# Strassen's seven block products in the up projections of a hybrid backbone's SwiGLU layers

## The chip, the cores and the metric

The kernel runs on one core of a Trainium2 chip, as one program. The metric is the device time of one execution in microseconds. A time is given as the median of several executions; the profile is of one execution, with its own time. Engines: TensorE (PE in the profile, its weight loads PEld), VectorE (DVE), ScalarE (ACT), GpSimd (POOL) and SyncE (SP), which issues nearly all DMAs.

## The reference

Two layers over 512 latent tokens and 256 context tokens, width 1024. Each layer is half a SwiGLU sub-layer, an attention mixer, and another half SwiGLU sub-layer, each modulated by vectors that come from a conditioning vector, and closed by a layer norm.

```python
def modulate(h, shift, scale):
    return h * (1.0 + scale) + shift

def swiglu(u, w_in, w_out):                 # w_in 1024 x 5632, w_out 2816 x 1024
    a, v = jnp.split(u @ w_in, 2, axis=-1)
    return (jax.nn.silu(a) * v) @ w_out

def ffn_sublayer(h, shift, scale, gate, w_in, w_out, g, b):
    y = swiglu(modulate(h, shift, scale), w_in, w_out)
    return layer_norm(ALPHA * h + FFN_RES * gate * y, g, b)
...
    for i in range(DEPTH):
        m_lat = jnp.split((silu_c @ w_mod[i] + b_mod[i])[:, None, :], N_MOD, axis=-1)
...
        h_lat = ffn_sublayer(h_lat, m_lat[0], m_lat[1], m_lat[2], ffn_w_in[i, 0], ffn_w_out[i, 0], ...)
...
        y_lat, y_ctx = neighborhood_attention(...)      # layer 0; window_gqa in layer 1
...
        h_lat = ffn_sublayer(h_lat, m_lat[6], m_lat[7], m_lat[8], ffn_w_in[i, 1], ffn_w_out[i, 1], ...)
```

Everything is float32. The context tokens go through the same sub-layers, except the last one.

## The kernel before, in words

Tokens lie in the free dimension: eight tiles `z` of 128 channels x 768 tokens hold the residual stream. A matmul of float32 precision is made of three in a shorter format (float32r): an operand x is split into `hi` (a rounded copy) and `lo` = x - hi, and `mm3` (L113 to L116) issues hi x hi, hi x lo and lo x hi into the same PSUM bank. The modulated input is kept split, in `uh` and `ul` (eight tiles each). Weights are streamed: `wunit` (L86) loads 1 MB in four raw quarter tiles of 128 x 512 through SP's queue (three raw buffers), ScalarE casts each to `hi` (L99) and GpSimd subtracts for `lo` (L100), into a ring of nine pairs.

`ffn` (L399) is called four times: 0a, 0b, 1a with two groups of tokens (512 latent, 256 context), and 1b with two groups of 256. The 2816 hidden columns are 22 tiles of 128, worked in eleven chunks of two. A chunk has three units of weights: two up units, each with the 128 `a` and the 128 `v` columns of one hidden tile, and one down unit. `av` (L407) does an up product for one group: `mmk` (L118) runs eight k-tiles times three matmuls for `a` into a bank "mm" and the same for `v` into a bank "c"; then Silu on ScalarE (L418), the product on VectorE (L419), and the split of the result into `gh` and `gl` (L420, L421). `down` (L423) runs for each of eight output tiles two k-tiles times three matmuls into one of three banks ("s", "s", "t"), and VectorE adds gate x result to `z` (`accumulate`, L394, L395). Chunk 0 is intertwined with the layer norm before it; chunk 9 does the first group alone and is repeated for the second group at the end (`late` and "r"); chunk 10 lets the next layer norm start early. Chunks 1 to 8 are the plain ones, called middle chunks here.

Beside the middle chunks runs a matrix-vector product in the background: `gemv_dve` (L155) computes modulation vectors of later stages on VectorE, one `tensor_tensor_reduce` on 128 x 256 per step (L172), with weight tiles `wt` in twelve slab buffers of a pool `sp` that the mixers use as well. `tick` (L192) emits steps: `rate` after each accumulate and before each up product. `behind` puts each step after the last accumulate in VectorE's queue.

The framework's planner turns this program into one fixed queue per engine, by data dependencies, buffers and its own estimate of times; so TensorE's queue has next chunk's up products between the down products of this one, and splits run ahead of their use as far as the ring lets them. At run time each engine takes its queue strictly in that order and waits where an operand or a buffer is not there yet. PSUM banks: "mm" 2, "s" 2, "c" 2, "t" 1, "o" 1.

Of the kernel before, what the change touches and what calls it, by code (L numbers as in the profile page):

```python
# [8 lines left out]
F32 = mybir.dt.float32  # L9
# [9 lines left out]
P = 128  # L19
# [12 lines left out]
SLABS = 12  # L32
RW = 63
# [3 lines left out]
def hybrid_kernel(ctx: ExitStack, tc: tile.TileContext, h0, cc, crow, wmod, wmodt, bmod, lnp, wst,  # L37
# [47 lines left out]

    def wunit(slabs=False, again=None):  # L86
# [4 lines left out]
        for q in range(4):  # L91
            nm = f"{i}_{q}" + ("" if again is None else "b")
            raw = wp.tile([P, 512], F32, tag="wr", name=f"wr{nm}", bufs=3)
            loaded[0] = nc.sync.dma_start(raw[:], wst[i, :, q * 512:(q + 1) * 512])
            if slabs:
                hi, lo = [sp.tile([P, 512], F32R, tag="slab", name=f"w{x}{nm}", bufs=SLABS) for x in "hl"]
            else:
                hi, lo = [wp.tile([P, 512], F32R, tag=f"w{x}", name=f"w{x}{nm}", bufs=9) for x in "hl"]
            nc.scalar.copy(hi[:], raw[:])  # L99
            nc.gpsimd.tensor_tensor(out=lo[:], in0=raw[:], in1=hi[:].bitcast(F32), op=ALU.subtract)  # L100
            hs.append(hi)
            ls.append(lo)
# [15 lines left out]
    def mmk(ps, w, m0, c0, c1):  # L118

        for k in range(DT):  # L120
            mm3(ps, kw(w, k, m0, m0 + P), [t[k][:, c0:c1] for t in (uh, ul)], k == 0, k == DT - 1)
# [23 lines left out]
    def gemv_bg(layer, ch):  # L145
        pieces = []
        for q in range(8):
            t = sp.tile([P, 1, 512], F32, tag="slab", name=f"wm{layer}_{ch}_{q}", bufs=SLABS)
# [6 lines left out]
    def gemv_dve(layer, t0, t1):  # L155

        cb = []

        def start():
            for i in range(4):  # L160
                t = sp.tile([P, 512], F32, tag="slab", name=f"cb{layer}_{t0}_{i}", bufs=SLABS)
                nc.sync.dma_start(t[:], crow[i // 2, i % 2:i % 2 + 1, :].broadcast_to([P, 512]))
                behind(nc.scalar.activation(t[:], t[:], AF.Silu), last_exp[0])
                cb.append(t)

        def products(acc, t, half):
            w = sp.tile([P, 512], F32, tag="slab", name=f"wt{layer}_{t}_{half}", bufs=SLABS)
            nc.sync.dma_start(w[:], wmodt[layer, t, half])
            for st in range(2):
                for q in range(2):  # L170
                    junk = t2(f"jk{layer}_{t}_{half}_{st}_{q}", "ln")
                    x = nc.vector.tensor_tensor_reduce(out=junk[:, 0:256], in0=w[:, q * 256:q * 256 + 256],  # L172
# [226 lines left out]
    def ffn(nm, groups, gt, mid, post, units=(), opened={}, head=None, apart=None):  # L399
# [34 lines left out]
        if mid is not None:  # L434
            mid()
# [673 lines left out]
```

## Time and profile before

| | |
|---|---|
| median of three executions | 2928.74 us (2925.1 to 2929.07) |
| profiled execution: its time | 2926.03 us |
| profiled execution: span from first to last instruction | 2924.2 us |
| mean granted TensorE clock | 0.983 of full speed |
| DMA | 286 MB, 98 GB/s over the span |
| ScalarE busy | 1033.0 us, 35% |

The profile's page gives busy time per engine, groups of instructions by source line (count, busy time, mean duration, and what ended the idle time before them) and DMA. Views of the trace cut this to a stretch of time, to one tile, or to single instructions in order. The shapes behind an arrow are partitions x elements. Matmuls overlap in the array, so the duration of a matmul is more than its share of TensorE's time; the distance from one start to the next is what counts. Over the middle chunks of 0a, 0b and 1a, 576 matmuls run in 100 us; of 1b, 849 do.

### The profile page before, as it was taken

The numbers are of one execution on the slowest core, as the hardware profiler recorded it, in microseconds if no ns is written. First come the engines' busy times: TensorE is split into PE (matmuls) and PEld (weight loads), VectorE is DVE, ScalarE is ACT, GpSimd is POOL, SyncE is SP. The second block draws the span as 40 slices with busy tenths as digits, with TensorE's granted clock in tenths as the row PEclk, the third lists the DMA queues.
The fourth block names the chain that finished last, engine by engine and source line by source line (L and its number), as shares of the span: only waits on it lengthen the run. The fifth ranks groups of instructions, "written<-read, shape, count | busy, mean of one in ns | idle before, by whom it ended". The sixth has DMA issues, their size and how long they took to land. (4 is left out here: it accounts for less than half of the span.)

```text
span 2924.2 us, 49325 instructions
## 1 busy us (share of the span) xinstructions
PE 2802.8 (96%) x18106; PEld 2470.4 (84%) x18106; DVE 1842.5 (63%) x5023; ACT 1033.0 (35%) x2122; POOL 1247.8 (43%) x1102
## 2 busy tenths in 40 slices
PE   8899999989999979999999899999998999899997
PEld 5788888888888869888888788888887777799997
DVE  3489994375545685767675757776358667733335
ACT  4122122266455452222223522121236655533333
POOL 4233232465433563332335623232456544644453
PEclk9999999999999989999999999999999999899998
DMA  7444442232211312343432324342321111233332
GB/s 290 147 148 145 134 138 61 85 89 80 66 50 52 108 60 87 109 126 109 122 96 87 112 87 121 108 125 73 87 85 55 51 37 30 76 94 96 97 108 81
DMA packets 165842, 286.05 MB, mean 98 GB/s; under 512 B 25952, under 2 KB 38368, under 8 KB 164576
## 3 DMA queue, kind: packets, MB, share of 16 engines
q1 hardware_dynamic: 165312, 282.76, 32.1%
q8 instruction: 142, 2.33, 0.3%
q14 instruction: 100, 0.82, 0.1%
q10 hardware_dynamic: 288, 0.14, 0.0%
HBM read 280.74 MB, written 6.48 MB: 98 GB/s over the span
## 5 line engine op out<-in xcount | busy, mean ns | idle before, releaser
L100 POOL TENSOR_TENSOR wl<-wr,wh 128x512 fp32r<-128x512 f32 x632 | 834.4, 1333 | 1226.7 <-ACT wh L99 1002.3
L99 ACT CAST wh<-wr 128x512 fp32r<-128x512 f32 x632 | 388.9, 620 | 738.4 <-DMA wr<-in_wst_dram 324.4
L172 DVE CUSTOM_DVE_ANT_0 jk<-wt,cb 128x256 f32<-128x256 f32 x960 | 489.3, 544 | 0.0
L395 DVE SCALAR_TENSOR_TENSOR z<-pd1a,gt,z 128x512 f32<-128x512 f32 (+1 forms) x168 | 103.0, 619 | 89.8 <-PE pd1a L116 89.6
L395 DVE SCALAR_TENSOR_TENSOR z<-pd0a,gt,z 128x512 f32<-128x512 f32 (+1 forms) x168 | 102.9, 618 | 83.9 <-PE pd0a L116 83.4
L395 DVE SCALAR_TENSOR_TENSOR z<-pd0b,gt,z 128x256 f32<-128x256 f32 (+1 forms) x176 | 105.0, 600 | 76.6 <-PE pd0b L116 76.5
L114 PE MATMUL pa0a<-uh,wh 128*128 128x512 f32 (+1 forms) x328 | 113.8, 347 | 14.8 <-ACT wh L99 10.9
L114 PE MATMUL pd0a<-gh0a,wh 128*128 128x512 f32 (+1 forms) x336 | 114.9, 345 | 2.9 <-DVE z L395 2.9
L114 PE MATMUL pd0b<-gh0b,wh 128*128 128x256 f32 (+1 forms) x352 | 116.7, 334 | 0.3 <-DVE z L395 0.3
L115 PE MATMUL pd0b<-gl0b,wh 128*128 128x256 f32 (+1 forms) x352 | 116.7, 332 | 0.0
L116 PE MATMUL pd0b<-gh0b,wl 128*128 128x256 f32 (+1 forms) x352 | 116.6, 332 | 0.0
L114 PE MATMUL pa1a<-uh,wh 128*128 128x512 f32 (+1 forms) x336 | 114.7, 341 | 1.2 <-DVE uh L259 1.2
L114 PE MATMUL pd1a<-gh1a,wh 128*128 128x512 f32 (+1 forms) x336 | 113.7, 342 | 1.3 <-DVE z L395 0.7
L114 PE MATMUL pv1a<-uh,wh 128*128 128x512 f32 (+1 forms) x336 | 114.6, 341 | 0.0
L115 PE MATMUL pv1a<-ul,wh 128*128 128x512 f32 (+1 forms) x336 | 114.5, 341 | 0.0
L115 PE MATMUL pa1a<-ul,wh 128*128 128x512 f32 (+1 forms) x336 | 114.3, 340 | 0.0
L116 PE MATMUL pd0a<-gh0a,wl 128*128 128x512 f32 (+1 forms) x336 | 114.3, 341 | 0.0
L115 PE MATMUL pd0a<-gl0a,wh 128*128 128x512 f32 (+1 forms) x336 | 114.3, 340 | 0.0
L116 PE MATMUL pv1a<-uh,wl 128*128 128x512 f32 (+1 forms) x336 | 114.2, 340 | 0.0
L115 PE MATMUL pd1a<-gl1a,wh 128*128 128x512 f32 (+1 forms) x336 | 114.2, 340 | 0.0
L116 PE MATMUL pa1a<-uh,wl 128*128 128x512 f32 (+1 forms) x336 | 114.2, 340 | 0.0
L116 PE MATMUL pd1a<-gh1a,wl 128*128 128x512 f32 (+1 forms) x336 | 114.0, 340 | 0.0
(882 smaller groups left out, 9238.2 us busy)
## 6 DMA issues: line engine op xcount, KB each, us to landing
wr<-in_wst_dram SPq DMA_DIRECT2D x632, 256.0 KB
wt<-in_wmodt_dram SPq DMA_DIRECT2D x240, 256.0 KB
wm<-in_wmod_dram SPq DMA_DIRECT2D x8, 1024.0 KB
nb<-yd SPq DMA_DIRECT2D x60, 128.0 KB
wr_0b<-in_wst_dram SPq DMA_DIRECT2D x19, 256.0 KB
wr_1b<-in_wst_dram SPq DMA_DIRECT2D x19, 256.0 KB
wr_2b<-in_wst_dram SPq DMA_DIRECT2D x19, 256.0 KB
wr_3b<-in_wst_dram SPq DMA_DIRECT2D x19, 256.0 KB
```

The lines of the kernel that those rows point to most:

```text
L99: nc.scalar.copy(hi[:], raw[:])
L100: nc.gpsimd.tensor_tensor(out=lo[:], in0=raw[:], in1=hi[:].bitcast(F32), op=ALU.subtract)
L114: nc.tensor.matmul(ps, a[0], b[0], start=first, stop=False)
L115: nc.tensor.matmul(ps, a[0], b[1], start=False, stop=False)
L116: nc.tensor.matmul(ps, a[1], b[0], start=False, stop=last)
L172: x = nc.vector.tensor_tensor_reduce(out=junk[:, 0:256], in0=w[:, q * 256:q * 256 + 256], in1=cb[2 * st + half][:, q * 256:q * 256 + 256], ...
L395: last[0] = nc.vector.scalar_tensor_tensor(out=zt(d, c0, c1), in0=pd, scalar=gt[:, d, st:st + 1], in1=zt(d, c0, c1), op0=ALU.mult, op1=ALU ...
```

## The change

In the middle chunks, the up product of a unit is written as a 2 x 2 block product: the weights A are cut in `a` and `v` columns times two halves of the contraction (k-tiles 0 to 3 and 4 to 7), the input B in the same two halves of the contraction times even and odd blocks of 128 tokens. Strassen's method (in Winograd's form) gets the four result blocks from seven block products in place of eight. Each product is four k-tiles of three matmuls with 384 columns (three blocks of 128 at a stride of 256; 256 columns in 1b).

The sums of the input are made once per FFN, after chunk 0 (`sums`): x1, x2 and x3 go, split, into tiles of a new pool; x4 takes the place of one block of `uh` and `ul`, which is saved to DRAM and brought back after chunk 8 (`restore`). The sums of the weights are made for each unit (`quarters`): s1, s2 on VectorE, s3, s4 on GpSimd, so seven pairs are split per unit in place of four. `seven` issues the products and combines them from PSUM on ScalarE, VectorE and, once, GpSimd. After each unit `tick(2 * rate)` is called, after each accumulate `tick(rate)`. In 1b's middle chunks `down` takes all 512 tokens as one group.

To make room: the ring has 8 pairs instead of 9, raw tiles are 5 instead of 3; the slab pool lives only outside the middle chunks ("S"), and a pool "T" only inside; the background gemv works on 512 columns per step, with two buffers for `wt`, half of the contraction after the other, and one addition at the end for all tiles in place of three small operations per tile; the two gate products at the start take their weights through the six `t2` buffers. The late chunk starts its contraction with k-tile 4. Where chunk 0 does its groups apart, its down unit is loaded again too.

```diff
+RING = 8
+RAWS = 5
...
     def gemv_dve(layer, t0, t1):
+        def products(t, half, cb):
+            w = ph["T"].tile([P, 512], F32, tag="wt", name=f"wt{layer}_{t}_{half}", bufs=2)
             nc.sync.dma_start(w[:], wmodt[layer, t, half])
             for st in range(2):
-                for q in range(2):
-                    junk = t2(f"jk{layer}_{t}_{half}_{st}_{q}", "ln")
-                    x = nc.vector.tensor_tensor_reduce(out=junk[:, 0:256], in0=w[:, q * 256:q * 256 + 256],
...
+                junk = t2(f"jk{layer}_{t}_{half}_{st}", "ln")
+                x = nc.vector.tensor_tensor_reduce(out=junk[:], in0=w[:], in1=cb[st][:], scale=1.0, scalar=0.0,
+                                                   op0=ALU.mult, op1=ALU.add, accum_out=acc[:, t - t0, half, st:st + 1])
+                behind(x, last[0])
+                yield
...
-        bg.append((8 * (t1 - t0), steps()))
+        bg.append((4 * (t1 - t0), steps()))
...
+        def sums():
+            saved = dp.tile([2, 4, P, n2], F32, name=f"sv{nm}")
+            for j in range(4):
+                for x, t in enumerate((uh, ul)):
+                    nc.sync.dma_start(saved[x, j].rearrange("p (a b) -> p a b", b=P), half(t[j], 1).bitcast(F32))
+                x1, x2, x3, x4 = [t2(f"x{nm}_{j}_{i}")[:, 0:n2] for i in range(4)]
...
+                k = j + 4
+                op(nc.vector, x1, (uh[j], 1), (uh[j], 0), ALU.subtract)
+                op(nc.vector, x1, x1, (ul[j], 1), ALU.add)
+                op(nc.vector, x1, x1, (ul[j], 0), ALU.subtract)
+                op(nc.gpsimd, x3, (uh[k], 1), (uh[j], 1), ALU.subtract)
+                op(nc.gpsimd, x3, x3, (ul[k], 1), ALU.add)
+                op(nc.gpsimd, x3, x3, (ul[j], 1), ALU.subtract)
+                op(nc.vector, x2, (uh[k], 1), x1, ALU.subtract)
+                op(nc.vector, x2, x2, (ul[k], 1), ALU.add)
+                op(nc.vector, x4, x2, (uh[k], 0), ALU.subtract)
+                op(nc.vector, x4, x4, (ul[k], 0), ALU.subtract)
+                for i, x in enumerate((x1, x2, x3)):
...
+                    nc.scalar.copy(hi, x)
+                    nc.vector.tensor_tensor(out=lo, in0=x, in1=hi.bitcast(F32), op=ALU.subtract)
+                    ts[i][j] = [as_half(hi), as_half(lo)]
+                nc.scalar.copy(half(uh[j], 1), as_half(x4))
+                nc.vector.tensor_tensor(out=half(ul[j], 1), in0=as_half(x4), in1=half(uh[j], 1).bitcast(F32), op=ALU.subtract)
...
+        def quarters():
...
+            out = [pair("a11", a11), pair("a12", a12)]
+            s1 = tt(nc.vector, 1, a21, a22, ALU.add)
+            s2 = tt(nc.vector, 2, s1, a11, ALU.subtract)
+            out += [pair("s2", s2), pair("s1", s1)]
+            s4 = tt(nc.gpsimd, 4, a12, s2, ALU.subtract)
+            s3 = tt(nc.gpsimd, 3, a11, a21, ALU.subtract)
+            return out + [pair("s4", s4), pair("s3", s3), pair("a22", a22)]
...
+        def seven(un, gh, gl):
...
+            def product(n, tag, b):
+                ps = bank(tag, f"p{n}{un}")
+                for k in range(4):
+                    mm3(as_half(ps[:, 0:n2]), [t[:, k * P:(k + 1) * P] for t in w[n]], b[k], k == 0, k == 3)
+                return ps[:, 0:n2]
...
+            nc.scalar.copy(va, product(0, "mm", b11))
+            op(sa, product(1, "o", b21), va)
+            nc.scalar.activation(sa, sa, AF.Silu)
+            op(va, product(2, "mm", ts[1]), va)
+            nc.scalar.copy(vb, product(3, "c", ts[0]))
+            op(sb, va, vb, eng=nc.gpsimd)
+            op(sb, product(4, "c", b22), sb)
+            nc.scalar.activation(sb, sb, AF.Silu)
+            op(va, product(5, "mm", ts[2]), va)
+            op(vb, va, vb)
+            op(va, va, product(6, "o", x4), ALU.subtract)
+            for h, (v, x) in enumerate(((va, sa), (vb, sb))):
+                op(v, v, x, ALU.mult)
+                nc.scalar.copy(half(gh, h), as_half(v))
+                op(half(gl, h), as_half(v), half(gh, h).bitcast(F32), ALU.subtract)
...
+            if not r and 0 < ci < NCH - 2:
+                gs = [[gp.tile([P, NT], F32R, tag="gs", name=f"g{x}{nm}_{ci}_{i}", bufs=6) for x in "hl"] for i in range(2)]
+                for i in range(2):
+                    seven(f"{nm}_{ci}_{i}", *gs[i])
+                    tick(2 * rate)
+                w = [None, None, wunit()]
+                if ci == NCH - 3:
+                    restore(saved)
+                for g in ([(0, NL, 0)] if nb == 2 else groups):
+                    down(w[2], f"{ci}", gs, g, True)
...
+            if ci == 0:
+                phase("T")
+                saved = sums()
```

137 lines of the change are left out of this document (90 added, 47 removed).

## The prediction

> **What bounds the kernel now.** I read the page first, for the engines' shares and the costliest groups.
>
> ```profile
> span 2924.2 us, 49325 instructions
> PE 2802.8 (96%) x18106; PEld 2470.4 (84%) x18106; DVE 1842.5 (63%) x5023; ACT 1033.0 (35%) x2122; POOL 1247.8 (43%) x1102
> ...
> L100 POOL TENSOR_TENSOR wl<-wr,wh 128x512 fp32r<-128x512 f32 x632 | 834.4, 1333 | 1226.7 <-ACT wh L99 1002.3
> L99 ACT CAST wh<-wr 128x512 fp32r<-128x512 f32 x632 | 388.9, 620 | 738.4 <-DMA wr<-in_wst_dram 324.4
> ```
>
> TensorE looks like the bound, but these are averages over unlike stages. So I took the stretches that hold only middle chunks, one in each of the four FFNs (0a, 0b, 1a, 1b in this order).
>
> ```profile
> core 0: us, PE busy (x) PEld busy (x) DVE busy (x) ACT busy (x) POOL busy (x), PEclk, DMA share, GB/s
> 200.00:400.00 200.00, 198.00 (x1138) 173.68 (x1137) 182.20 (x658) 43.35 (x80) 64.97 (x48) 1.00 0.46 139
> 1200.00:1400.00 200.00, 200.00 (x1151) 175.96 (x1150) 146.91 (x481) 44.25 (x80) 63.94 (x48) 1.00 0.39 116
> 1800.00:2000.00 200.00, 200.00 (x1152) 175.92 (x1151) 144.77 (x480) 45.02 (x80) 63.47 (x48) 1.00 0.39 116
> 2600.00:2800.00 200.00, 200.00 (x1696) 200.00 (x1696) 73.34 (x142) 60.92 (x117) 89.12 (x70) 1.00 0.32 93
> ```
>
> A middle chunk has 288 matmuls (192 up, 96 down), half of 512 columns and half of 256. By the counts of these rows it takes 50.6 us in 0a, 50.0 in 0b and 1a, 34.0 in 1b, where all have 256 columns. The mean step from one matmul to the next is 200/1151 = 0.174 us, and 200/1696 = 0.118 us in 1b. TensorE has no idle time there, so what the change takes off TensorE comes off the end, if no other engine takes its place. In 0a VectorE is 91% busy, in 0b and 1a 73%; why that is so shows in the next rows, of 0a and of 0b, and in the least, median and greatest time of the same operation.
>
> ```profile
> L172 DVE CUSTOM_DVE_ANT_0 jk<-wt,cb 128x256 f32<-128x256 f32 x236 | 113.5, 517 | 0.0
> L395 DVE SCALAR_TENSOR_TENSOR z<-pd0a,gt,z 128x512 f32<-128x512 f32 x31 | 23.1, 744 | 2.4 <-PE pd0a L116 2.1
> L395 DVE SCALAR_TENSOR_TENSOR z<-pd0a,gt,z 128x256 f32<-128x256 f32 x32 | 15.3, 477 | 4.7 <-PE pd0a L116 4.7
> L187 DVE TENSOR_SCALAR mod<-ga,bmod_sb 128x2 f32<-128x2 f32 x29 | 12.3, 423 | 0.2
> L185 DVE TENSOR_TENSOR ga<-ga 128x4 f32<-128x4 f32 x29 | 8.8, 303 | 0.1
> L186 DVE TENSOR_TENSOR ga<-ga 128x2 f32<-128x2 f32 x29 | 7.7, 267 | 0.2
> ```
> ```profile
> L172 DVE CUSTOM_DVE_ANT_0 jk<-wt,cb 128x256 f32<-128x256 f32 x160 | 81.0, 538 | 0.0
> L421 DVE TENSOR_TENSOR gl0b<-sl0b,gh0b 128x256 fp32r<-128x256 f32 x8 | 11.5, 1436 | 5.8 <-ACT gh0b L420 5.8
> L185 DVE TENSOR_TENSOR ga<-ga 128x4 f32<-128x4 f32 x20 | 5.8, 290 | 0.1
> ```
> ```profile
> L172 DVE CUSTOM_DVE_ANT_0 jk<-wt,cb x236: 405/415/1510, 199.8 to 399.7; 128x256 f32<-128x256 f32 x118
> ```
>
> Over the whole span, the same kind of operation with one operand in PSUM:
>
> ```profile
> L419 DVE TENSOR_TENSOR sl0a<-pv0a,sl0a 128x512 f32<-128x512 f32 x22 | 15.1, 686 | 34.0 <-PE pv0a L116 33.9
> L419 DVE TENSOR_TENSOR sl1b<-pv1b,sl1b 128x256 f32<-128x256 f32 x42 | 17.8, 424 | 100.0 <-PE pv1b L116 95.6 <-ACT sl1b L418 4.4
> ```
>
> A product of the background gemv takes 0.415 us, yet its mean is 0.517: some take 1.5. The timeline of VectorE and of GpSimd at one place shows what these wait for.
>
> ```profile
> 1807.10 0.47 DVE L395 SCALAR_TENSOR_TENSOR z<-pd1a,gt,z 128x256 f32<-128x256 f32 x1
> 1808.54 1.50 DVE L172 CUSTOM_DVE_ANT_0 jk<-wt,cb 128x256 f32<-128x256 f32 x1
> 1810.39 0.41 DVE L172 CUSTOM_DVE_ANT_0 jk<-wt,cb 128x256 f32<-128x256 f32 x1
> 1810.73 0.41 DVE L172 CUSTOM_DVE_ANT_0 jk<-wt,cb 128x256 f32<-128x256 f32 x1
> 1811.08 0.15 DVE L186 TENSOR_TENSOR ga<-ga 128x2 f32<-128x2 f32 x1
> 1811.84 0.21 DVE L187 TENSOR_SCALAR mod<-ga,bmod_sb 128x2 f32<-128x2 f32 x1
> ```
> ```profile
> 1807.01 1.32 POOL L100 TENSOR_TENSOR wl<-wr,wh 128x512 fp32r<-128x512 f32 x1 [0.47 <-PE pv1a L115]
> ```
> ```profile
> 1808.28 1.47 POOL L100 TENSOR_TENSOR wl<-wr,wh 128x512 fp32r<-128x512 f32 x1
> ```
>
> The product of 1808.54 reads two tiles in SBUF and ends at 1810.04, 0.29 us after GpSimd's split ends at 1809.75: it had to wait for it. The accumulate of 1807.10, which reads PSUM and SBUF, ran through a split in its usual 0.47. So a GpSimd tensor_tensor stops VectorE's operations on two SBUF tiles, and not those that read PSUM. The price per split in 0a: 236 x (0.517 - 0.415) = 24.1, L187 29 x (0.423 - 0.21) = 6.2, L185 and L186 29 x (0.303 + 0.267 - 0.30) = 7.8, together 38 us over 48 splits, **0.79 us**. In 0b: 160 x (0.538 - 0.415) = 19.7, L185 20 x (0.290 - 0.15) = 2.8, L421 8 x (1.436 - 0.424) = 8.1, together 30.6 over 48, **0.64 us**.
>
> **TensorE.** A unit has 96 up matmuls, 48 x 768 columns; seven products of four k-tiles by three terms are 84 of 384 columns (256 in 1b). 384 is the mean of 512 and 256, so a step is 0.174. A chunk is 168 + 96 = 264 steps: 45.8 us. In 1b down becomes one group, 48 steps of 512 columns at 2 x 0.174 - 0.118 = 0.23, so 168 x 0.118 + 48 x 0.23 = 30.9. Over eight chunks that would take 39 us off 0a, 34 off 0b, 34 off 1a and 25 off 1b: 132 us. I take three blocks of 128 as no dearer than a row of 384; were each 128 as dear as a 256-column step, 0.354, the method would lose outright, but nothing in the rows suggests it.
>
> **GpSimd.** Splits go from 12 to 18 per chunk (seven per unit in place of four, four for down). Added are two weight sums and one 384-column sum per unit: 24 operations for 12.
>
> ```profile
> L100 POOL TENSOR_TENSOR wl<-wr,wh 128x512 fp32r<-128x512 f32 x36 | 46.0, 1294 | 56.0 <-ACT wh L99 37.5 <-PE pv1b L115 12.4 <-PE pv1b L116 4.1
> L283 POOL TENSOR_TENSOR aql<-aql,sql 128x256 f32<-128x256 f32 x16 | 12.4, 773 | 22.2 <-ACT sql L361 21.9
> ```
>
> That is 22 x 1.294 + 2 x about 1.05 = 30.6 us per chunk: room under 45.8, hardly any under 30.9 (22 x 1.294 + 2 x 0.8 = 30.1 there). ScalarE has 18 casts of 0.62 and six copies or Silus per unit of at most 0.62: under 19 us, so it binds nowhere.
>
> **VectorE, without waits.** The next operation starts about 0.07 before one ends (1810.39 to 1810.73 is 0.34 for 0.41). Per chunk: 16 accumulates, 8 x (0.67 + 0.41) = 8.6. Per unit ten operations on 384 columns, five with PSUM and five on SBUF alone, each between 0.424 and 0.686, so 0.555 less 0.07: 20 x 0.485 = 9.7. Two weight sums per unit on 512 columns: 4 x 0.615 = 2.5. Together 20.8. A gemv product has now 512 columns: 0.415 + (0.686 - 0.424) = 0.677, less 0.07, 0.61. There are 192, 160 and 128 of these in 0a, 0b, 1a (half as many as before), at 40 per chunk in 0a (rate 2) and 20 in 0b and 1a (rate 1); the three small operations per modulation tile go.
>
> **With waits.** 24 operations of GpSimd at 0.64 to 0.79 are 15.4 to 19.0 us; I take 0.70, 16.8, about the middle, since the share of two-SBUF work stays near that of 0b while VectorE is as full as in 0a.
> - 0b: 20.8 + 12.2 + 16.8 = 49.8 (48.4 to 52.0) against TensorE's 45.8: VectorE is late next. Eight chunks 398, before 400: -2 (-13 to +16).
> - 0a: 4.8 chunks with products, 20.8 + 24.4 + 19.0 = 64.2, and 3.2 at TensorE's 45.8, are 455; spread evenly, 166 + 117 + 192 x 0.70 = 417. I take 436, halfway, as VectorE's order is planned ahead but late products slip; before 405: +31 (+12 to +50).
> - 1a: 6.4 x 49.8 + 1.6 x 45.8 = 392, before 400: -8 (-17 to +6).
> - 1b: GpSimd 30.1, and the 14 two-SBUF operations of VectorE, each of which can hold it up by 0.29 (256 columns, as above) to 0.55 (512), at most 5.1: 30.9 to 35.2, taken at 32.5. 260, before 272: -12 (-25 to +9).
> Sum +9.
>
> On this the Trainium skill ("SBUF — State Buffer", section "SBUF: two separate sides") says that the pair of ports shared by VectorE and GpSimd is an exclusive lock, kept for the whole instruction, also by a VectorE operation with two SBUF inputs. The trace agrees that one blocks the other; but 0.29 us after the split for an operation of 0.41 says that not all of it is held up. By the rule taken whole, the time would be that of the third rival below.
>
> **Beside the chunks.** Before the first Strassen chunk, 44 VectorE operations (44 x 0.485 = 21 us), 12 of GpSimd and 16 of ScalarE form sums and splits. Down of chunk 0 covers most: 96 steps are 16.7 us (11 in 1b). What must come after chunk 0's last up matmul is four casts and four subtractions of x4, about 4 us. Were none covered, 21 us per FFN; I take 5, so 20 us (0 to 84). Eight saves and eight restores per FFN go through SP's queue, past the weight loads.
>
> ```profile
> SPq L168 <- DVE ga L172: 447.2, 164, 5.8
> ```
> ```profile
> L168 SPq DMA_DIRECT2D wt<-in_wmodt_dram x20: 327/328/328, 1312.8 to 1396.4; - x20
> ```
>
> 16 x 0.33 = 5 us of issue, covered by raw tiles that are five deep. The gemv's weight tile falls from a share of twelve slabs to two of its own: VectorE never waited for it (idle 0.0 in L172), but SP did wait for VectorE. If a load arrives late, the accumulates queue behind the product and TensorE behind their banks: nothing to 60 us (480 products are 240 tiles, by 0.25 us each). Bank "o" takes products 2 and 7 of a unit, so VectorE must have emptied the seventh within one product of the next unit, 12 x 0.174 = 2.1 us; a gemv product of 1.50 ahead of it in the queue still leaves room for one operation. Ring 8 for 9 and six tiles for twelve under the first gate's gemv shorten loads ahead; chunk 0 of 0b and 1b loads and splits its down weights twice, 4 x 1.33 us of a GpSimd that is otherwise a third busy. None can gain, since buffers only fall; I take 6 for all. The other order of k in the late chunk costs nothing, its cover is chunk 8's down, 16.7 us for eight restores. Together +9 + 20 + 6 = +35. The profiled run took 2926.03 us, 1.8 beyond its span and 2.7 under the median of 2928.74: **2961 us**.
>
> **Rivals.**
> 1. *TensorE stays the bound* (faster). For it: in 0a VectorE is 91% busy and TensorE lost only 1%, so a nearly full VectorE costs little. Against: the waits grow with GpSimd's work. It decides where a GpSimd operation costs VectorE about 0.53: there 0b needs 20.8 + 12.2 + 12.8 = 45.8, so 0b and 1a give -34 each, 0a evenly spread 385, -20, 1b -15: -103, with the 26 beside 2849. At 0b's own 0.64 it is 0a +17, 0b -13, 1a -17, 1b -12: 2927. The rival is what lies between, its middle 2888.
> 2. *The weight tile's two buffers*: 60 for 6, and sums uncovered, 84 for 20: 2961 + 118 = 3079. For it: SP's 447 us on these products. Against: VectorE has never waited for a landing yet.
> 3. *The two engines line up one after the other*, each operation in its full duration: 0b 30.6 + 10 x 0.555 + 4 x 0.686 + 20 x 0.677 = 52.4, 419; 0a 4.8 x 66.0 + 147 = 463; 1a 409; 1b 30.1 + 10 x 0.424 + 4 x 0.686 = 37.1, 297. That is 1588 for 1477: +111 + 26, 3063. Against it: the 0.29.
> 4. *No saving*: a moving operand in three blocks costs more than 0.174. At 0.20 TensorE's chunk is 50.3, and 0b, 1a and 0a's light chunks follow: about 2980.
>
> **How the numbers follow.** Forecast 0.45 (its own range 2915 to 3005), rival 1 0.34, rival 2 0.08, rival 3 0.10, rival 4 0.03. The range 2860 to 3050 leaves out the best part of rival 1, most of rival 2 and half of rival 3, together under 2 in 10. About 0.2%, 6 us, is what a measurement of this kernel can tell from no change. Faster 0.36: rival 1, and 0.02 from the forecast's low edge; same 0.07, from that edge too; slower 0.57, all else.
>
> **What would show it.** Right: in 0b VectorE over 95% busy, TensorE 90 to 97% instead of 100, chunks of 47 to 52 us, 0a's first five chunks near 60, L172's successor with a mean far over 0.677, 1b's GpSimd over 90%. Wrong: middle chunks of 46 us in 0b with TensorE at 100% (rival 1), product waits that end on a DMA (rival 2), chunks over 52 (rival 3), steps over 0.18 us with no idle time (rival 4).

## The result and the profile after

| | before | after |
|---|---|---|
| median (four executions each) | 2928.55 us | 3155.01 us (3148.95 to 3161.61) |
| profiled execution: time, span | 2926.03, 2924.2 us | 3161.61, 3159.8 us |
| mean granted TensorE clock | 0.983 | 0.945 |

The ratio is 1.0776 (95% interval 1.0752 to 1.0801): slower by 226 us, where 32 were forecast and at most 121 allowed for. First the page of after: the engines' line, and its three costliest groups, which answer to the product and to most of the splits of before.

```profile
span 3159.8 us, 48012 instructions
PE 2825.9 (89%) x16954; PEld 2497.9 (79%) x16954; DVE 2330.5 (74%) x4333; ACT 1216.5 (38%) x2514; POOL 1895.8 (60%) x1542
...
L98 POOL TENSOR_TENSOR wl<-wr,wh 128x512 fp32r<-128x512 f32 x376 | 515.7, 1389 | 316.1 <-ACT wh L97 273.6
L187 DVE CUSTOM_DVE_ANT_0 jk<-wt,cb 128x512 f32<-128x512 f32 x480 | 502.6, 1066 | 8.5 <-DMA wt<-in_wmodt_dram 4.3
L98 POOL TENSOR_TENSOR wl_s<-S,wh_s 128x512 fp32r<-128x512 f32 x256 | 379.8, 1504 | 87.8 <-ACT wh_s L97 82.3
```

PE has 1152 matmuls fewer and is yet busy 23 us longer, at a lower granted clock. VectorE is busy 488 us more, GpSimd 648. A product that takes 0.67 us alone has a mean of 1.066. Now the stretches that hold the eight middle chunks of 0a, 0b, 1a and 1b, in this order:

```profile
core 0: us, PE busy (x) PEld busy (x) DVE busy (x) ACT busy (x) POOL busy (x), PEclk, DMA share, GB/s
140.00:612.00 472.00, 394.55 (x2045) 359.07 (x2044) 396.86 (x686) 128.41 (x238) 279.01 (x191) 0.93 0.41 119
1250.00:1678.00 428.00, 394.71 (x2073) 358.61 (x2072) 369.18 (x605) 129.43 (x244) 280.07 (x196) 0.94 0.40 113
1871.00:2294.00 423.00, 391.13 (x2067) 358.01 (x2068) 358.45 (x572) 130.35 (x245) 285.49 (x196) 0.95 0.38 108
2776.00:3062.00 286.00, 260.75 (x1722) 236.83 (x1723) 192.53 (x252) 120.61 (x246) 252.89 (x198) 0.98 0.34 98
```

A chunk takes about 60 us in 0a (480 with the part of the first one ahead of this stretch), 53.4 in 0b, 52.9 in 1a, 35.7 in 1b, where 45.8 (30.9 in 1b) is TensorE's own work. In 0b no engine is full: PE 92% at 0.94 of its clock, VectorE 86%, GpSimd 65%. From the starts of the matmuls in 0b's stretch, some 360 us are steps at full rate, 15 to 20 are what steps at half the clock take more, and 45 to 50 are waits (how a step that is both slow and late is divided is a matter of choice). Against before, the middle chunks are 138 us longer (75, 27, 23, 13); the rest of the loss, about 100, lies outside them, above all between chunk 0 and the first block products.

Where VectorE's time goes in 0b, by groups (busy, mean):

```profile
L187 DVE CUSTOM_DVE_ANT_0 jk<-wt,cb 128x512 f32<-128x512 f32 x148 | 151.2, 1034 | 2.6 <-ACT cb L198 1.9 <-DMA wt<-in_wmodt_dram 0.7
...
L538 DVE TENSOR_TENSOR gl0b<-y0b,gh0b 128x384 fp32r<-128x384 f32 x32 | 41.7, 1328 | 0.1
L538 DVE TENSOR_TENSOR y0b<-y0b,y0b 128x384 f32<-128x384 f32 x32 | 37.6, 1181 | 1.0
L538 DVE TENSOR_TENSOR y0b<-y0b 128x384 f32<-128x384 f32 x16 | 18.3, 1147 | 0.9
L509 DVE TENSOR_TENSOR S<-wr,wr 128x512 f32<-128x512 f32 x15 | 14.1, 942 | 14.9 <-DMA wr<-in_wst_dram 14.9
L509 DVE TENSOR_TENSOR S<-S,wr 128x512 f32<-128x512 f32 x15 | 12.0, 800 | 0.4
...
L538 DVE TENSOR_TENSOR y0b<-p10b,y0b 128x384 f32<-128x384 f32 x15 | 8.2, 546 | 0.0
```

All six groups with two SBUF operands are stretched; the one that reads PSUM (p10b) is not: its mean is 0.546. With 0.55 us taken for 384 columns, 0.615 for a weight sum and 0.672 for a product, the excess is 148 x 0.362 + 32 x 0.778 + 32 x 0.631 + 16 x 0.597 + 15 x (0.327 + 0.185) = 116 us of standing still, for 196 operations of GpSimd: 0.59 us each. How it hits TensorE is seen at the end of one unit, in the timeline of VectorE and GpSimd:

```profile
1500.91 0.55 DVE L538 TENSOR_TENSOR y0b<-p50b,y0b 128x384 f32<-128x384 f32 x1
1501.56 0.72 DVE L538 TENSOR_TENSOR y0b<-y0b 128x384 f32<-128x384 f32 x1
1501.83 1.58 POOL L509 TENSOR_TENSOR S<-wr,wr 128x512 f32<-128x512 f32 x1
1502.39 1.44 DVE L538 TENSOR_TENSOR y0b<-y0b,y0b 128x384 f32<-128x384 f32 x1
1503.38 4.70 POOL L98 TENSOR_TENSOR wl_s<-S,wh_s 128x512 fp32r<-128x512 f32 x3
1503.75 0.54 DVE L538 TENSOR_TENSOR y0b<-y0b,p60b 128x384 f32<-128x384 f32 x1
1504.32 1.06 DVE L538 TENSOR_TENSOR y0b<-y0b,y0b 128x384 f32<-128x384 f32 x1
1505.31 3.18 DVE L538 TENSOR_TENSOR gl0b<-y0b,gh0b 128x384 fp32r<-128x384 f32 x2
```

Seven operations that need about 3.5 us take 7.6. The accumulates and the next unit's evacuations stand behind them in VectorE's queue. TensorE's longest waits in 0b's stretch (us in total, times, longest) are of that kind:

```profile
PE p10b L136 <- DVE y0b L538: 15.1, 13, 2.3
PE pd0b L137 <- DVE gl0b L538: 4.1, 7, 0.6
```

The first is bank "o": product 2 of a unit (its tile is `p1`, counted from 0) waits until VectorE has emptied product 7 (`p6`) of the unit before.

### The profile page after: what moved, and what is told of

Its sections match the earlier page's. It is cut to its first block, busy times and chain, and to the rows that moved or that the text cites. A ratio compares the mean times of both kernels' runs of the same rounds, so it can differ in the third digit from the quotient of the medians.

```text
span 3159.8 us, 48012 instructions
## 1 busy us (share of the span) xinstructions
PE 2825.9 (89%) x16954; PEld 2497.9 (79%) x16954; DVE 2330.5 (74%) x4333; ACT 1216.5 (38%) x2514; POOL 1895.8 (60%) x1542
## 3 DMA queue, kind: packets, MB, share of 16 engines
q1 hardware_dynamic: 288320, 296.40, 32.5%
## 4 chain that ended last, share of the span: by engine, by line
PE 52%; DVE 30%; issue 7%; DMA 5%; POOL 3%; ACT 3%; SPq 1%; DVEq 0%; POOLq 0%; ACTq 0%
DVE jk L187 8%; DVE z L411 3%; DMA wr<-in_wst_dram 3%; DVE y0b L538 2%; DVE y1a L538 2%; PE pd0b L137 1%; PE pd1a L137 1%; DVE S L509 1%; DVE y1b L538 1%; PE pd1a L138 1%; PE pd0b L138 1%; PE wo L697 1%; DVE y0a L538 1%; PE pd1a L136 1%; PE o L697 1%
## 5 line engine op out<-in xcount | busy, mean ns | idle before, releaser
L98 POOL TENSOR_TENSOR wl<-wr,wh 128x512 fp32r<-128x512 f32 x376 | 515.7, 1389 | 316.1 <-ACT wh L97 273.6
L187 DVE CUSTOM_DVE_ANT_0 jk<-wt,cb 128x512 f32<-128x512 f32 x480 | 502.6, 1066 | 8.5 <-DMA wt<-in_wmodt_dram 4.3
L98 POOL TENSOR_TENSOR wl_s<-S,wh_s 128x512 fp32r<-128x512 f32 x256 | 379.8, 1504 | 87.8 <-ACT wh_s L97 82.3
L98 POOL TENSOR_TENSOR wl_a<-wr,wh_a 128x512 fp32r<-128x512 f32 x192 | 276.3, 1443 | 222.6 <-ACT wh_a L97 170.9
L97 ACT CAST wh<-wr 128x512 fp32r<-128x512 f32 x376 | 226.4, 619 | 236.4 <-DMA wr<-in_wst_dram 41.1
L97 ACT CAST wh_s<-S 128x512 fp32r<-128x512 f32 x256 | 155.8, 619 | 325.6 <-DVE S L509 100.1
L97 ACT CAST wh_a<-wr 128x512 fp32r<-128x512 f32 x192 | 118.2, 619 | 198.4 <-issue 58.9
L509 POOL TENSOR_TENSOR S<-wr,S 128x512 f32<-128x512 f32 x64 | 85.7, 1340 | 123.2 <-DVE S L509 92.5
L509 DVE TENSOR_TENSOR S<-wr,wr 128x512 f32<-128x512 f32 x64 | 68.1, 1065 | 82.3 <-DMA wr<-in_wst_dram 82.3
L704 POOL TENSOR_SCALAR p<-p,l 128x512 f32<-128x512 f32 x64 | 44.5, 697 | 118.7 <-DVE l L802 108.6
```

Of the source, the lines that this page charges most:

```text
L97: nc.scalar.copy(hi[:], src[:])
L98: nc.gpsimd.tensor_tensor(out=lo[:], in0=src[:], in1=hi[:].bitcast(F32), op=ALU.subtract)
L187: x = nc.vector.tensor_tensor_reduce(out=junk[:], in0=w[:], in1=cb[st][:], scale=1.0, scalar=0.0, op0=ALU.mult, op1=ALU.add, accum_out=acc ...
L509: eng.tensor_tensor(out=t[:], in0=a[:], in1=b[:], op=o)
L704: nc.gpsimd.tensor_scalar(out=p, in0=p, scalar1=r, scalar2=0.0, op0=ALU.mult, op1=ALU.add)
```

## The experiments

Times in us, each of one execution beside before on the same chip (2922.92 to 2929.65 there); the stage columns, from the traces, run from the start to the first `pq`, from the first `pa0b` to the first `pa1a`, from there to the first `vw`, and from the first `pa1b` to the end of the last matmul. The four executions of after lie 12.7 us apart and those of before on the several chips 6.7, so a difference of some 10 us between two single runs says little.

| kernel | time | 0a | 0b | 1a | 1b |
|---|---|---|---|---|---|
| before | 2928.55 | 615 | 569 | 569 | 404 |
| after | 3155.01 | 720 | 625 | 613 | 439 |
| e1 no sums of the input | 3070.84 | 685 | 604 | 589 | 428 |
| e2 product 7 in bank c | 3133.72 | 717 | 606 | 600 | 448 |
| e3 no background products | 2944.86 | 617 | 564 | 565 | 439 |
| e4 before, no background products | 2914.73 | 607 | 576 | 567 | 403 |
| e5 no GpSimd in weight splits | 2883.80 | 641 | 540 | 545 | 394 |
| e8 products spread evenly | 3095.98 | 680 | 619 | 592 | 441 |
| e9 old up projection in the new frame | 2953.36 | 638 | 577 | 570 | 401 |
| e10 before, splits done twice | 3038.20 | 682 | 592 | 588 | 404 |
| e11 before, no GpSimd in splits | 2895.71 | 604 | 563 | 563 | 401 |
| e12 = e2 + e8 | 3087.55 | 685 | 609 | 588 | 443 |
| e13 = e1 + e2 + e3 | 2849.29 | 590 | 542 | 537 | 418 |
| e14 products with one operand | 3006.59 | 652 | 574 | 570 | 445 |
| e15 = e2 + operand in PSUM | 3094.93 | 699 | 590 | 586 | 457 |
| e16 = e15 + e8 + slabs for the first gate | 3030.58 | 631 | 596 | 584 | 454 |
| e17 = e16 + sums under chunk 1 | 3020.63 | 640 | 601 | 577 | 442 |
| e18 = e16 without the sums | 2930.19 | 609 | 565 | 560 | 432 |
| e19 = e16, products in down only | 3041.04 | 637 | 602 | 587 | 451 |

**First round: the sums, the bank, the products.** After the result my theory was that three things stack up: the sums of the input stand uncovered (A), bank "o" chains two units (B), and the products meet more of GpSimd (C). The rival to C was that the block method costs as much without them.

```diff
e1:
-                saved = sums()
+                ts[i][j] = [half(t[j], 0) for t in (uh, ul)]   # for each i, j
e2:
-            op(va, va, product(6, "o", x4), ALU.subtract)
+            op(va, va, product(6, "c", x4), ALU.subtract)
e3, e4:
-        bg.append((4 * (t1 - t0), steps()))
+        nc.vector.memset(acc[:], 0.01)
```

> Leaves out the sums of the input: no x1 to x4, no save and no restore; the products read the plain blocks of uh and ul, and everything else stays. Theory A (the four transitions from chunk 0 to the first Strassen chunk are exposed, because 44 VectorE operations per FFN stand in VectorE's queue between the accumulates of chunk 0's down): TensorE's idle and slow-clock time there, some 20 to 35 us per FFN, goes, so 70 to 110 us less than 3155, near 3065; the middle chunks stay at 53 us in 0b and 1a. Rival (the transition is late for other reasons, the layer norm before it or the first weights): under 25 us less, above 3130.

> One word changed: the seventh product of a unit goes to a bank of the pair c instead of the single bank o. Theory B (TensorE waits at the second product of the next unit for VectorE to empty the seventh out of the same bank; these waits add up to 15 us in 0b, 11 in 1a, 8 in 0a, 2 in 1b): 20 to 36 us less than 3155, and the waits of p1 on y go. Rival (VectorE is what is late, and the wait moves to the next bank that it must empty): within 10 us of 3155.

> Leaves out the background matrix-vector products on VectorE and the loads of their weights; the modulation vectors that they give are constants. To be compared with the kernel before without the same products. Theory C (VectorE and GpSimd together are too full in the middle chunks): 0b's and 1a's middle chunks fall from 53 us to 46 to 47, 0a's from 60 to 46 to 48, 1b's stay at 35.6; in all about 160 less, 2995, which is still above the kernel before without them, by the transitions. Rival (banks and order cost the same whatever VectorE has to do): middle chunks stay above 50 us, 3090 or more.

> The kernel before without the same background products: the measure for the run without them in the changed kernel. Theory C and its rival expect the same, since TensorE had no idle time in the middle chunks: 2900 to 2929, up to 10 us less in 0a.

84, 21 and 210 us went away, against the median of after. Before, the same edit as e3's took 8 us off (2922.92 on that chip). e3's 210 is more than the 160 expected, e2's 21 is the low end of what was expected, with 1b 9 us longer. So the products cost 8 us before and some 200 in the new kernel, where there are half as many of twice the width. Without them the block method is 30 us slower than before, not 226. Yet GpSimd's hold on VectorE is still there: a stretch of e3's 0b, and the group that ends a unit in it.

```profile
1145.00:1515.00 370.00, 367.18 (x2089) 347.81 (x2088) 239.30 (x313) 130.41 (x241) 262.38 (x195) 1.00 0.27 77
```
```profile
L517 DVE TENSOR_TENSOR gl0b<-y0b,gh0b 128x384 fp32r<-128x384 f32 x32 | 46.3, 1484 | 3.4 <-PE pd0b L137 3.3
```

The subtraction stands longer than in after (1.484 for 1.328), and TensorE waits only 2.9 us of the 370.

**Who makes them dear.** In e5 the splits' low halves leave GpSimd; e11 does that to before. e10 gives before as many GpSimd operations as the new kernel has. e8 moves products from 0a's full chunks to its light ones. e9 keeps the frame and drops the block method.

```diff
e5, e11:
-        nc.gpsimd.tensor_tensor(out=lo[:], in0=src[:], in1=hi[:].bitcast(F32), op=ALU.subtract)
+        nc.scalar.copy(lo[:], src[:])
e8:
-        rate = -(-sum(n for n, _ in bg) // (20 * (NCH - 3)))
+        rate = sum(n for n, _ in bg) / (20.0 * (NCH - 3))      # tick carries the fraction over
e9:
-            if not r and 0 < ci < NCH - 2:
+            if False:
e10 (before, middle chunks only):
+            for _ in range(2):
                 nc.gpsimd.tensor_tensor(out=lo[:], in0=raw[:], in1=hi[:].bitcast(F32), op=ALU.subtract)
```

> The changed kernel, but the low half of every weight split is a plain ScalarE copy of the tile instead of GpSimd's subtraction (so the low half is not the remainder, and the products are not the reference's). GpSimd keeps its three operations per unit. Theory (GpSimd's two-SBUF operations hold up VectorE, and through VectorE's queue TensorE): the middle chunks of 0b and 1a go from 53 us to 46 to 48, those of 0a from 60 to 52 or less, those of 1b from 35.6 to 31 to 32; with some 170 us fewer in all, about 2960 to 3010. Rival (VectorE's own work and TensorE's halved clock after short waits make the chunk, whoever causes the waits): the middle chunks of 0b stay at 51 us or more, and the time over 3090. ScalarE has then 40 copies of 0.6 us a chunk, 25 us, which bounds neither.

> The changed kernel with the background products of the modulation spread evenly over the eight middle chunks of a stage (24 per chunk in 0a, where it was 40 in the first 4.8 chunks; 16 in 1a for 20; 0b is unchanged at 20). Theory (what a product costs grows where VectorE is already full): the middle chunks of 0a take 56 to 58 us in place of 60 on average, 15 to 35 us fewer, 1a 0 to 5 fewer: about 3120 to 3140. Rival (each product costs the same wherever it stands): 3150 to 3160.

> The changed kernel with its smaller rings, its pools by phase, its products of 512 columns on two buffers and its order of the late chunk, but with the middle chunks' up projections done the old way, without block products and block sums. Theory (the loss comes from the block method, not from the housekeeping): 2915 to 2945, as before. Rival (the two buffers of the modulation's weight tile, the ring of eight or the split done twice cost much): over 2960.

> The kernel before, with each GpSimd subtraction of the middle chunks' weight splits done twice (the second gives the same values): 24 operations of GpSimd per chunk in place of 12, as many as the changed kernel has, and nothing else of it. Theory (a GpSimd operation costs a full VectorE about 0.65 us): 0a's chunks with products of rate 2 go from 50.6 to about 58, 20 to 45 us in all; 0b and 1a have VectorE at 44 of 50 us and lose 0 to 15 each; 1b 0 to 10: 2945 to 2990. Rival (GpSimd's work costs VectorE nothing of weight): within 5 us of before. If it is over 3000, GpSimd's operations alone explain most of the loss.

> The kernel before, with the low half of every weight split a plain ScalarE copy in place of GpSimd's subtraction (the low half is not the remainder). It is the control of the same edit in the changed kernel, which went to 2884. Theory (before, TensorE is busy without a break in the middle chunks of 0b and 1a, so GpSimd's hold on VectorE costs it little): 2895 to 2925, and the block method is then worth some 10 to 40 us where GpSimd leaves VectorE alone. Rival (the edit is worth the same to both): under 2800.

e5 went to 2883.8, further than the theory had it, and its control e11 to 2895.7: with GpSimd's splits out of the way the block method is worth 12 us (16 against the runs of before beside them), all overheads paid, which for single runs is hardly clear of their spread. One stretch of e5, nearly eight chunks of 0b, and the group that ends a unit:

```profile
1154.00:1518.00 364.00, 364.00 (x2072) 346.71 (x2071) 276.29 (x606) 205.69 (x392) 60.62 (x48) 1.00 0.45 133
```
```profile
L538 DVE TENSOR_TENSOR gl0b<-y0b,gh0b 128x384 fp32r<-128x384 f32 x32 | 17.7, 555 | 0.5 <-ACT gh0b L556 0.4
```

TensorE has no gap, at full clock, 364/2072 = 0.176 a step; the subtraction is back from 1.328 to 0.555. e10 lost 108, where I expected 60 at most: 66 in 0a, that is 0.69 us for each of 96 added operations, 23 and 19 in 0b and 1a, nothing in 1b, which has no products. This is the price that the prediction took, without any block product. e8 gained 59, more than expected: 40 in 0a, 21 in 1a, where 0 to 5 were expected and nothing here explains the rest. e9 is 24 above before, between theory and rival; by the stages 0a is 23 longer and 0b 8: the frame does cost. One place is the first gate, where TensorE in e9 waited for the weights that now pass through six tiles (us in total, times, longest, from 60 to 110 us; before had no wait there):

```profile
PE gm L155 <- DMA wm<-in_wmod_dram: 2.8, 1, 2.8
```

That line holds only 2.8 of the 23; the rest was not traced to a line.

**The operand.** e14 and e15 ask whether the products cost by their time or by their second SBUF operand. e12 and e13 ask whether the single gains add.

```diff
e14:
-                x = nc.vector.tensor_tensor_reduce(out=junk[:], in0=w[:], in1=cb[st][:], ...)
+                x = nc.vector.tensor_reduce(out=acc[:, t - t0, half, st:st + 1], in_=w[:], axis=AX.X, op=ALU.add)
e15 (with e2; product 2 in bank "s", down in "s", "s", "mm"):
-                    behind(nc.scalar.activation(t[:], t[:], AF.Silu), last_exp[0])
+                    s = bank("to"[st], f"cs{layer}_{t0}_{half}_{st}")
+                    behind(nc.scalar.activation(s[:], t[:], AF.Silu), last_exp[0])
```

> The changed kernel with the seventh product in bank c and the background products spread evenly: both edits compute the same values. If the two gains (21 and 59) stand apart: about 3075. If they remove the same wait, 3090 to 3110. In neither case is it below before.

> The changed kernel without the background products, without the block sums of the input (the products read plain blocks instead), and with the seventh product in bank c: what is left is the seven products, the weights' sums and splits. The products' values are not the reference's. Theory (the saving on TensorE is there, 126 us, and the three things hide it): before without background products was 2915, less 126 and with 24 of the smaller buffers 2813; by adding the three single gains 2840. So 2810 to 2850. Rival (the chunks wait on something else still, such as GpSimd's 24 operations): 2870 or more.

> The changed kernel with each background product replaced by a VectorE sum over the same weight tile, 512 columns, which reads one SBUF operand and writes one column (the modulation's values are not the reference's). The number of operations, their places and their loads stay. Theory (VectorE's operations with two SBUF operands stand still while GpSimd reads; an operation with one does not): the mean of one falls from 1.07 us to 0.55 to 0.70, the middle chunks of 0b from 53 to 47 to 50, 0a's from 60 to 50 to 54, and the time to 3020 to 3090. Rival (it is the products' own time and place in VectorE's queue): the mean stays at 0.9 or more, or the time over 3120.

> The changed kernel with the same products and the same values, but the modulation's broadcast operand (two tiles of 512 columns) lies in two PSUM banks and not in SBUF, so that a background product reads one operand from SBUF and one from PSUM. The two banks come free because product 2 goes to the bank s, product 7 to c, and the down projection of a middle chunk cycles s, s, mm. Theory (VectorE stands still in its operations with two SBUF operands while GpSimd reads): the product's mean falls from 1.07 us to 0.65 to 0.80, the middle chunks of 0b from 53 to 47 to 50, and of 3134 (the kernel with the seventh product in c) 80 to 140 are gone: 2990 to 3055. Rival (the product's own time is what costs): mean over 0.95, or the time over 3100.

e12 kept 67 of 80, between its two expectations. e13 came out 9 above what the single gains add up to, with a 0b in which TensorE never waits:

```profile
1096.00:1468.00 372.00, 372.00 (x2135) 354.59 (x2134) 236.99 (x318) 130.49 (x241) 256.57 (x192) 1.00 0.25 71
```

372/2135 = 0.174 us a step. GpSimd is as busy as in after (69%, where after had 65%), the subtraction that ends a unit takes 1.511 on the mean, and it does no harm where VectorE has slack (64% busy). e14 gave 148 of the 210, 13 us below its range, with a mean of 0.675 for its sum and about 48 us for a chunk of 0b, which supports the theory. e15 keeps the same operation on the same values. The products of after (in 0b) and of e15 (all), least, median and greatest time, and e15's groups at that line:

```profile
L187 DVE CUSTOM_DVE_ANT_0 jk<-wt,cb x148: 672/787/1783, 1251.9 to 1677.0; 128x512 f32<-128x512 f32 x148
```
```profile
L187 DVE CUSTOM_DVE_ANT_0 jk<-wt,cs x480: 666/679/690, 118.1 to 2157.6; 128x512 f32<-128x512 f32 x160
```
```profile
L187 DVE CUSTOM_DVE_ANT_0 jk<-wt,cs 128x512 f32<-128x512 f32 x480 | 314.1, 680 | 33.9 <-DMA wt<-in_wmodt_dram 32.8 <-DVE z L412 0.3 <-DVE ga L187 0.2
L187 DVE DVE_READ_ACCUMULATOR2_ANT ga<- 128x1 f32 x480 | 39.3, 82 | 0.0
```

Not one of the 480 stands still for GpSimd any more, as the theory had it, and yet only 39 us went where 80 to 140 were expected; the middle chunks of 0b went to 50, the upper end. Where the rest stayed, the groups of e15 in its 0b show (from 1228 to 1628 us):

```profile
L539 DVE TENSOR_TENSOR gl0b<-y0b,gh0b 128x384 fp32r<-128x384 f32 x32 | 39.8, 1262 | 3.5 <-ACT gh0b L557 2.6
L539 DVE TENSOR_TENSOR y0b<-y0b,y0b 128x384 f32<-128x384 f32 x32 | 34.9, 1111 | 1.0
```

The operations that end a unit still read two SBUF tiles, and still stand. TensorE's longest waits in that stretch name those, and no background product:

```profile
PE pd0b L137 <- DVE gl0b L539: 8.6, 7, 1.4
PE pd0b L136 <- ACT gh0b L557: 7.6, 7, 2.2
```

That alone does not explain e15, for in e14 the same subtraction takes 1.317 and e14 gained 148. New waits come up as well: VectorE waits 33 us for `wt` and its two buffers, but in e14 it waits 36. What sets e15 apart is TensorE's queue. By the starts of its matmuls in 0b, the other banks made the planner order the products anew: the second products of two units stand together, 24 matmuls, where after and e14 have them apart. 1b, which has no background products, hints at the price of such an order: it takes 457 in e15, 445 in e14 and 448 with bank "c" alone. e14's sum also needs no second instruction to read the accumulator (39 us of VectorE in e15, above). How the 88 us between e14 and e15 divide among these was not tried, so e15 is no clean measure of what the operand is worth. e16 to e19 have e15's banks and its order of the products too.

**A version to keep.** e16 to e19 keep what paid, look for the sums, and for the place of the products.

```diff
e16 (e15, e8 and this):
-            t = t2(f"wm{layer}_{ch}_{q}").rearrange("p (a b) -> p a b", a=1)
+            t = ph["S"].tile([P, 1, 512], F32, tag="slab", name=f"wm{layer}_{ch}_{q}", bufs=SLABS)
e17 (e16 and this; the sums are steps after chunk 1's up products, x4 is formed between its up and down,
     the background products are spread over seven chunks):
-            if not r and 0 < ci < NCH - 2:
+            if not r and 1 < ci < NCH - 2:
e18: e16 with e1's edit
e19 (e16 and this):
-                    tick(2 * rate)
```

> The kernel of the PSUM operand, with the products spread evenly as well and the first gate's weight tiles in twelve slabs again, as before. All edits keep the values. Theory: 30 to 60 below the kernel of the PSUM operand for the even spread (less than the 59 alone, since products are cheaper), 10 to 20 for the first gate: 2935 to 3000. Rival (the sums and GpSimd's other waits leave it there): over 3010.

> The kernel with all three edits, and the sums of the input formed during chunk 1, which is done the old way: its four up products cover the sums that go to tiles of their own, and only the sum that is written in place stands between chunk 1's up and down. Seven chunks instead of eight use the block method, which gives up 16 us of the 126. Theory (the sums cost 84 because nothing covers them): 84 - 16 - 10 to 20 = 45 to 60 below the kernel with all three edits: 2880 to 2950. Rival (covered sums take as much from VectorE elsewhere): within 20 of it or above.

> The kernel with the PSUM operand, the even spread and the twelve slabs (3031), and without the block sums of the input (plain blocks are read instead, so the products' values are not the reference's). Theory (the sums are a term of their own, 84): 2935 to 2955, and what is then left over the kernel without sums and without background products (2849) is the products' own time, 90 to 105. Rival (with less on VectorE the sums cost less): 2965 or more.

> The kernel with the PSUM operand, the even spread and the twelve slabs (3031), with the background products issued between the steps of the down projection alone, and none between the two units of a chunk. The values stay. Theory (a product queued ahead of a unit's evacuations holds their banks and TensorE): 3000 to 3020. Rival (what stays is the chain from a unit's seventh product through the gate to down, and VectorE's total): 3025 to 3050.

e16 gained 64 more, within the 40 to 80 that its two edits were expected to bring, and missed its range by 31, since e15 had missed. e17 gained 10, as the rival had it, no more than two single runs can differ by: under chunk 1 the sums are not free either, and VectorE is 93% busy there. A stretch of e17's chunk 1 in 0b:

```profile
1130.00:1170.00 40.00, 27.25 (x160) 25.00 (x159) 37.37 (x52) 10.43 (x23) 28.45 (x19) 0.79 0.31 93
```

e18 shows the sums at 100 us in e16, a term of their own. It is level with before (2929.34), so in this order of TensorE's queue even a free set of sums would only have broken even with GpSimd's splits where they are. e19 is 10 slower, as its rival had it: the place of the products was not it. No kernel that keeps all the work came below before; e17, the fastest of them with block products, is 3.2% above its run of before.

## Why the prediction was wrong

The direction was right, the size was not: 226 us over the median of before for the 32 forecast (+35 in the sum, which starts at the profiled run). Of the 201 us that the span grew beyond the sum's +35, 129 lie in the middle chunks (138 for +9: 0a 44 over its term, 1a 31, 0b 29, 1b 26) and some 72 beside them (98 for 26). Step by step:

- *TensorE saves 132 us.* Right. The 1152 matmuls fewer are worth 126 at full rate, and the 1323 matmuls with three blocks of 128 in e13's stretch have a mean step of 0.174, which refutes rival 4.
- *A GpSimd operation costs VectorE 0.70.* Right in size: 0.59 in 0b, and 0.69 in 0a of e10. The Trainium skill ("SBUF — State Buffer", section "Who interferes with whom") says that a VectorE instruction with at most one SBUF input, outside the two-port modes, does not contend with GpSimd; e15's 666/679/690 agrees.
- *"VectorE is late next"*, 49.8 us per chunk in 0b. This is the step that failed. VectorE's busy time came out below it (369.2/8 = 46.1) and the chunk above it (53.4). I took the larger of two engines' sums for the chunk's time, as if each could use all its idle time. In after neither could: VectorE and TensorE hand over in fixed order, and in 0b's stretch VectorE waited for TensorE's down products, for weights and for GpSimd's sum (lines below), while TensorE waited for VectorE. The runs show that it takes both loads on VectorE: without the products TensorE waits 2.9 us in e3's stretch, without GpSimd's splits not at all in e5's, with both 45 to 50. So it is not enough that an operation between two units stands: 62 of 0b's 116 us fall on the ends of the units and the weight sums, but these stand as long in e3 and e13 and cost TensorE next to nothing there. Why two loads that leave VectorE 14% idle cannot be fitted in is argued from the fixed order, not shown by a run that changes it. The weights' arrival is not it, since VectorE's wait for them is longer in e5 and e13 (23.2 and 27.7) with TensorE never waiting.

```profile
DVE z L411 <- PE pd0b L138: 25.8, 45, 3.2
DVE S L509 <- DMA wr<-in_wst_dram: 14.9, 5, 3.4
DVE y0b L538 <- POOL y0b L538: 10.6, 3, 7.9
```

- *1b at 32.5 a chunk.* It took 35.7, above the 35.2 taken for the worst, though it has no background products. GpSimd is 88% busy there, and TensorE's longest waits are for the ends of the units (9.9 us for `gl1b`, 5.8 for `gh1b`) and for the splits of the weight sums.
- *0a at 436.* It took about 480: the same fault, with 40 products a chunk on top. I took halfway to the even spread, and e8's 40 us there are what the front-loading costs.
- *"Down of chunk 0 covers most"* of the sums, 5 us per FFN. Wrong: 84 in all by e1, 100 by e18, or 21 to 25 per FFN, as much as none of it covered. The layer norm's operations, chunk 0's accumulates and the sums all want VectorE at that time. From 1790 to 1871 us of after, where the stage 1a begins:

```profile
1790.00:1871.00 81.00, 65.06 (x324) 56.20 (x322) 73.58 (x131) 31.15 (x63) 46.29 (x38) 0.87 0.19 56
```

  VectorE 91% busy, TensorE 80% at a clock of 0.87. The cover that I named was TensorE's time, not VectorE's.
- *6 us for all the rest.* Bank "o" alone is 21 (e2), the frame 24 (e9), most of it in 0a. The bank was reasoned with a product ahead of the evacuation, not with GpSimd stopping the operations ahead of it.
- *Rivals.* 1 fell: VectorE's waits do reach TensorE. 2 is refuted in its mechanism, since the products waited 4.3 us for `wt`, but its 84 for bare sums was right. 3 came nearest in the chunks, 52.4 for 53.4 in 0b, though not because VectorE was busy all that time: it was 86% busy, where the sign for a right forecast was over 95%. No rival added the bare sums to it: 3063 + 64 is 3127.

The sum as it was measured, from after downwards: bank 21, PSUM operand 39, even spread and first gate 64, sums 100: 2930. The last 81, down to e13's 2849, hold the products' own time and what the changed banks and TensorE's other order cost; in 1b, without products, e18 takes 432 and e13 418. e13 is 65 under before without products (2915), of TensorE's 126. The terms depend on their order.

One wait was left alone. GpSimd makes one of the unit's sums, in one queue with its splits, and VectorE waited for it 53.8 us in after (12 times, 8.0 at most). No run gave that sum to VectorE, so what it is worth stays open; in e3's 0b VectorE waited 12.0 us for it and TensorE lost next to nothing.

## What to carry to other kernels

Fewer matmuls buy little if what replaces them goes to the engines that empty TensorE's banks. Where two engines hand work to each other in a fixed order, the larger of their sums is a lower bound for the time, not the time: here 46.1 and 45.8 us of work made chunks of 53.4, and taking either load off VectorE, the products or GpSimd's hold, brought 0b's chunk back to within 1 us of TensorE's own time. A GpSimd operation with SBUF operands cost a VectorE in demand about 0.6 to 0.7 us here, paid by whichever operation with two SBUF operands is next. A cover has to be idle time of the engine that does the covered work. An edit that moves tiles to other banks can reorder a whole queue; the order has to be read from the trace before a gain is put down to the edit.

## What the runs showed of the hardware

The granted clock falls after quite short waits. In 0b of after the longest wait of TensorE from 1256 to 1300 us is 2.4 us, it ends at 1261.62, and the clock is at half in all of the 3 us from 1263:

```profile
1258.00:1262.00 4.00, 1.63 (x10) 1.34 (x9) 3.44 (x3) 0.91 (x2) 4.00 (x3) 1.00 0.31 89
1263.00:1266.00 3.00, 3.00 (x11) 3.00 (x10) 0.00 (x0) 0.72 (x2) 3.00 (x4) 0.50 0.07 20
```

```profile
1263.18 0.52 PE L138 MATMUL p50b<-T0b_2h,wl_s 128*128 128x384 f32 x1
1263.50 0.52 PE L136 MATMUL p50b<-T0b_3h,wh_s 128*128 128x384 f32 x1
```

Matmuls of 384 columns start 0.32 us apart in it, where 0.174 is the step in an undisturbed chunk. The Trainium skill ("TensorE: Matmul & The Clock Gate", Part 1) has the clock fall after an idle window of about 3.4 us; here 2.4 us of one wait was enough. In the trace's clock records of after, which know 1.00 and 0.50 alone, all changes lie on a grid of 3.41 us. In the 3.41 us before 47 of the 52 falls TensorE was busy for less than half of the time, and after the first 30 us only five such stretches, of 0.47 and more, left the clock at 1.00. So it is waits that fill about half of such a stretch that cost clock here.

The mean granted clocks, 0.983 and 0.945, make 99 us at half the clock in before and 348 in after. Worked out from the starts of all matmuls, of the 236 us by which the span grew, some -130 are work at full rate, some +75 to +90 what steps at half the clock take more, and some +280 waits; the division is an estimate. So the added waits cost about a quarter to a third of their length again in slower steps. In the stretches of e5 and e13, where TensorE has no waits, the clock is 1.00.
